# Keys of the memory for the second layer: from a one-pass float32 product to three float32r passes over split rows

## The chip, the cores and the metric

The kernel runs on one core of a Trainium2 chip. The metric is the device time of one execution in microseconds (us). The five parts of the core that the profile shows are PE (matmul, with its weight loads as PEld), DVE, ACT, POOL, and the queue of SP, which issues most of the DMAs.

## What is computed

The reference is an encoder trunk of two layers over 256 rows of 1024 channels. The first layer mixes by a bidirectional state-space layer (S5) with a gated linear unit behind it, the second by dilated attention. Each layer then attends into 256 rows of a memory, with normalised queries and keys, and ends with an MLP:

```python
for i in range(DEPTH):                       # DEPTH = 2
    hn = rms_norm(h, norm_mix[i])
    h = h + (s5_mixer(hn, ...) if i % 2 == 0 else dilated_attention_mixer(hn, ...))
    h = h + memory_cross_attention(rms_norm(h, norm_xattn[i]), rms_norm(mem, norm_mem[i]), ...)
    h = h + sq_relu_mlp(rms_norm(h, norm_mlp[i]), mlp_w1[i], mlp_w2[i])
# in memory_cross_attention, mem_n is the normalised memory:
kv = (mem_n @ w_kv).reshape(bsz, mlen, 2, MEM_HEADS, MEM_HEAD_DIM)
k = rms_norm(kv[:, :, 0], g_k)
v = kv[:, :, 1]
```

The products `mem_n @ w_kv` of both layers depend on the memory alone. There are four of them, each 256 x 1024 by 1024 x 1024: keys and values of layer 0, keys and values of layer 1.

## The kernel before

The four products are written by `memory_part(layer, q, ...)`, where q is 0 for keys and 1 for values. It has two ways to multiply. With one operand tile it calls `gemm32` (L240 to L252): plain float32 matmuls of 128x512 at L248, 32 of them for one product, each of which the trace shows as two records. The weights come by `weight_raw` (L234) into the pool of four `raw` tiles. With two operand tiles, a high and a low part in float32r, it calls `gemm`: per half of a weight block (256 rows of 512 columns) `weight_half` loads the same `raw` tile (L193), ACT casts it to `whi` (L161), DVE makes the rest `wlo` (L162), and `unit_mms` issues twelve matmuls of 128x512, three for each operand block: high by high (L207), high by low (L208), low by high (L209). One product is 96 such matmuls and eight halves.

The order of the program is this. First comes the S5 stage, in eight chunks. In each, DVE makes input weights (`s5_weigh_in`, transposed by PE at L1042 and copied by ACT at L1044), PE drives the states (`drive`, L1081), DVE scans them (`scan`, L1096 to L1113, with decays R that ACT writes at L1091 and L1092), ACT copies them (L1116, L1117), PE makes impulse responses (`impulse`, L1144, from `wk`, which ACT fills at L1135 to L1138; the result `kx` goes to DRAM at L1154 and comes back as M at L1160, issued from ACT's queue), and `read` multiplies states, W and M (L1173, L1176), applies a gelu (G, L1179) and transposes (L1185). Behind the S5 stage, still under its PSUM pools, stand `load_gains` (L121), `bias_rows` (L483 to L496, with two small matmuls at L489, its copies at L490, and DMAs on SP's queue), the load of x, and three products in plain float32: keys of layer 0, values of layer 0, keys of layer 1.

Then the PSUM pools change from two, five and one banks to four and four. In the new ones the transposed memory rows of layer 1, `mT[1]`, are split into the two tiles `mp` (pool `m1`). The values of layer 1 follow in three passes, then the gated unit (`glu`). The keys of each layer are normalised by `key_norms` (L350 on ACT, L354 on POOL), which the `hook` calls after each half of the values; the keys of layer 0 are transposed (L379) during the gated unit's first part, those of layer 1 only in the first cross attention.

Tile, the framework, orders each engine's instructions when the program is built: those written earlier go first, and those written later fill in where the earlier ones can't run yet and where their buffers are free. So the float32 products, written behind the S5 stage, stand between its instructions in PE's order. Pools on a stack reuse each other's memory: `m1` lies where the pool `s5` lay, and the split weights `whi` and `wlo` (pool `wq`) partly where the pool `s5m` lay. In the built program the instructions that first write `mp` wait for the last matmul of the S5 stage that reads from `s5`, and the first cast to `whi` waits for the last users of `s5m`.

Of the kernel before, what the change touches and what calls it, by code (L numbers as in the profile page):

```python
# [1251 lines left out]
def trunk(tc, a, stages=("s0", "x0", "m0", "d1", "x1", "m1")):  # L1252
    with ExitStack() as ctx:
        k = Trunk(ctx, tc, a)
        nc = tc.nc
        seq = [q for q in ("s0", "x0", "m0", "d1", "x1", "m1") if q in stages]
        first = {"x": "norm_xattn", "m": "norm_mlp", "d": "norm_mix"}
        xin = lambda: nc.sync.dma_start(k.h, a["x"][0].rearrange("(t p) c -> p t c", p=P))

        def store(nb):  # L1260
            for t in range(2):
                cs = slice(nb * 512, (nb + 1) * 512)
                (nc.sync, nc.scalar)[t].dma_start(a["out"][t * P:(t + 1) * P, cs], k.h[:, t, cs])

        after = {}
        for n, q in enumerate(seq):
            after[q] = k.norm_after(first[seq[n + 1][0]], int(seq[n + 1][1])) if n + 1 < len(seq) else \
                (store, None)
        late = ("norm_mix", "norm_xattn", "norm_mlp", "xattn_q_gain", "attn_q_gain", "attn_k_gain")
        early = ("norm_mem", "xattn_k_gain")  # L1270
        kvp0 = tc.alloc_tile_pool(name="kv0", bufs=1)
        right = lambda n: ctx.enter_context(tc.tile_pool(name=n, bufs=1, side="right"))
        krp = tc.alloc_tile_pool(name="kr", bufs=1)
        kv = [[krp.tile([P, 2, D], F32, name="k%d" % q), (kvp0, right("v1"))[q].tile([P, 2, D], F32, name="v%d" % q)]
              for q in range(2)]
        keys = [None, None]
        if "s0" in seq:
            kvt = tc.alloc_tile_pool(name="kvt", bufs=1)
            with k.banks(2, 5, 1):
                with tc.tile_pool(name="s5", bufs=1) as ph:  # L1280
                    with tc.tile_pool(name="s5p", bufs=1) as pr:
                        k.load_gains(pr, early, nc.sync)
                        k.s5_load(pr, kv[0][1], kv[1])
                        k.s5_params(pr)
                        mT = [k.memory_in(0, kvt, kv[0][1])]
                        k.s5_norm(ph, kv[0][0].rearrange("p a b -> p (a b)"))
                        k.s5_tables(ph)
                        k.s5_b(ph)
                        turns = k.s5_turns(pr, ph, k.h.rearrange("p t c -> p (t c)"))
                        k.s5_weigh_in(ph, 0)  # L1290
                        k.s5_c(ph, pr)
                        k.s5_skip(ph, pr)
                        k.s5_input(ph)
                        mr = k.row_rstd(kv[0][1], "mem")
                        mT.append(k.memory_in(1, kvt, kv[0][1]))
                    gT = k.new_x()
                    with tc.tile_pool(name="s5m", bufs=1) as mp:
                        k.s5(mp, ph, turns, gT)
                        k.load_gains(mp, late, nc.sync)
                        k.bias_rows()  # L1300
                xin()
                k1 = right("k1")
                k.wq = right("wq")
                k0 = tc.alloc_tile_pool(name="k0", bufs=1, side="right")
                k.memory_part(0, 0, kv[0][0], mT[:1], mr, k.kvw)
                k.memory_part(0, 1, kv[0][1], mT[:1], mr)
                k.memory_part(1, 0, kv[1][0], mT[1:], mr)
        else:
            with k.banks(4, 4), tc.tile_pool(name="kvt", bufs=1) as kvt:
                k.load_gains(kvt, early, nc.sync)  # L1310
                k.load_gains(kvt, late, nc.sync)
                k.bias_rows()
                mem = kvt.tile([P, 2, D], F32, tag="mem", name="mem")
                k.memory_load(mem)
                mr = k.row_rstd(mem, "mem")
                k1 = right("k1")
                k.wq = right("wq")
                k0 = tc.alloc_tile_pool(name="k0", bufs=1, side="right")
                for q in range(2):
                    if "x%d" % q in seq:  # L1320
                        mT = [k.memory_in(q, kvt, mem)]
                        for i in range(2):
                            k.memory_part(q, i, kv[q][i], mT, mr)
                        keys[q] = k.key_parts(q, k.key_norms(q, kv[q][0], kvt), (k0, k1)[q])
                xin()
        with k.banks(4, 4):
            if "s0" in seq:
                m1 = tc.alloc_tile_pool(name="m1", bufs=1)
                parts = [m1.tile([P, KT, S], F32R, tag="mp%d" % q, name="mp") for q in range(2)]
                for q in (slice(0, 4), slice(4, 8)):  # L1330
                    k.split(parts[0][:, q], parts[1][:, q], mT[1][:, q])

                kn = {}

                def norms(nb):
                    kn[nb] = k.key_norms(nb, kv[nb][0], k0)

                k.memory_part(1, 1, kv[1][1], parts, mr, hook=norms)
                k.glu(gT, after["s0"][0], lambda: keys.__setitem__(0, k.key_parts(0, kn[0], k0)))
                m1.release()  # L1340
                kvt.release()
                st = after["s0"][1]
            else:
                done, st = k.norm_after(first[seq[0][0]], int(seq[0][1]))
                done(0)
                done(1)
            krp.release()
            for q in seq:
                done, nst = after[q]
                L = int(q[1])  # L1350
                if q[0] == "x":
                    with tc.tile_pool(name="xa", bufs=1) as ph:
                        def fill():
                            if q == "x0" and "s0" in seq:
                                keys[1] = k.key_parts(1, kn[1], k1)

                        vals = [ph.tile([P, 2, D], F32R, tag="v%d" % i, name="vp") for i in range(2)]
                        k.memory_attention(L, st["x"], st["r"], (keys[L], vals, kv[L][1]), done, ph, fill)
                    if L == 0:
                        k0.release()  # L1360
                        kvp0.release()
                elif q[0] == "m":
                    k.mlp(L, st["x"], st["r"], done)
                elif q[0] == "d":
                    k.dilated_attention(st["x"], st["r"], done)
                st = nst if q[0] != "s" else st
        if "x0" not in seq:
            k0.release()
            kvp0.release()
# [25 lines left out]
```

## Time and profile before

| what | us |
| --- | --- |
| median of 3 runs (lowest to highest) | 1068.58 (1065.11 to 1069.62) |
| the profiled execution, its own time | 1063.82 |
| its span, first to last instruction | 1062.0 |
| PE busy in the span | 1009.4 (95%) |
| DVE, ACT, POOL busy | 693.7, 576.6, 211.2 |

The mean granted clock of TensorE over the span is 0.988. The page divides the span by engine; the timeline gives instructions in order of time, merged where they repeat; a window row gives the stretch, its length, the busy time of PE, PEld, DVE, ACT and POOL with the number of instructions in brackets, the granted clock (1.00 is 2.4 GHz, 0.50 is 1.2 GHz), the busy share of the DMA engines and the GB/s that they moved. In a timeline the columns are start, duration, engine, line, operation, destination and sources, count, and in square brackets the idle time before it with what ended it. Times count from the span's start.

### The profile page before, as it was taken

How to read it: one execution, taken by the hardware profiler on the slowest of the kernel's cores; microseconds unless marked ns; L12 is line 12 of the kernel's file. 1: busy time of each engine (PE TensorE's matmuls, PEld its weight loads, DVE VectorE, ACT ScalarE, POOL GpSimd, SP SyncE). 2: the span in 40 equal slices, each digit the busy share in tenths (PEclk: the TensorE clock that was granted, in tenths of full speed). 3: DMA queues.
4: the chain of work that ended last, by engine and by line, in shares of the span. 5: the costliest groups of instructions: out<-in, count | busy, mean ns of one | idle time of the engine just before them, and what ended most of it. 6: DMA issues, size and time to landing. Idle time of an engine off the chain costs nothing. (4 is left out here: it accounts for less than half of the span.)

```text
span 1062.0 us, 17010 instructions
## 1 busy us (share of the span) xinstructions
PE 1009.4 (95%) x6591; PEld 829.6 (78%) x6591; DVE 693.7 (65%) x1108; ACT 576.6 (54%) x1030; POOL 211.2 (20%) x186
## 2 busy tenths in 40 slices
PE   4878889989999999999989999999999999999998
PEld 4545446568898988999778878878788989889996
DVE  7889996366686645444667777778747775544444
ACT  7545444675675644444545656667535655444443
POOL 3999880030000110000220030000200001100000
PEclk9999899999999999999999999999999999999999
DMA  9322233465533455555555555554325244555552
GB/s 197 106 90 71 64 125 104 153 209 178 172 129 130 169 187 175 190 191 181 178 179 179 159 168 178 157 163 141 127 90 174 104 156 163 178 190 188 188 186 101
DMA packets 98429, 163.80 MB, mean 154 GB/s; under 512 B 16704, under 2 KB 27116, under 8 KB 98092
## 3 DMA queue, kind: packets, MB, share of 16 engines
q1 hardware_dynamic: 89052, 158.84, 47.5%
q10 hardware_dynamic: 9296, 3.87, 1.4%
q8 instruction: 52, 0.85, 0.3%
q14 instruction: 29, 0.24, 0.1%
HBM read 160.70 MB, written 3.83 MB: 155 GB/s over the span
## 5 line engine op out<-in xcount | busy, mean ns | idle before, releaser
L162 DVE TENSOR_TENSOR wlo<-raw,whi 128x1024 fp32r<-128x1024 f32 x264 | 331.1, 1255 | 237.4 <-ACT whi L161 233.9
L161 ACT CAST whi<-raw 128x1024 fp32r<-128x1024 f32 x264 | 276.7, 1048 | 225.9 <-PE psa L209 143.0
L207 PE MATMUL psa<-whi,xs 128*128 128x512 f32 x448 | 178.2, 398 | 0.5 <-ACT sg L1220 0.5
L209 PE MATMUL psa<-whi,xs 128*128 128x512 f32 x448 | 177.2, 396 | 0.0
L208 PE MATMUL psa<-wlo,xs 128*128 128x512 f32 x448 | 176.9, 395 | 0.0
L292 POOL TENSOR_TENSOR sq<-rl 128x512 f32<-128x512 f32 x32 | 40.1, 1252 | 531.5 <-ACT rl L291 531.5
L279 PE MATMUL psb<-xs,whi 128*128 128x256 f32 x512 | 145.1, 283 | 0.0
L281 PE MATMUL psb<-xs,whi 128*128 128x256 f32 x512 | 145.0, 283 | 0.0
L283 PE MATMUL psb<-xs,wlo 128*128 128x256 f32 x512 | 144.9, 283 | 0.0
L209 PE MATMUL psa<-whi,hl 128*128 128x512 f32 x256 | 101.6, 397 | 0.0
L208 PE MATMUL psa<-wlo,hh 128*128 128x512 f32 x256 | 101.5, 397 | 0.0
L207 PE MATMUL psa<-whi,hh 128*128 128x512 f32 x256 | 101.4, 396 | 0.0
L248 PE MATMUL psa<-raw,mT 128*128 128x512 f32 x192 | 95.1, 639 | 5.7 <-ACT k L334 5.7
L279 PEld LDWEIGHTS psb<-xs,whi 128*128 128x128 f32 x512 | 98.2, 192 | 0.9 <-DVE xs L184 0.4
L281 PEld LDWEIGHTS psb<-xs,whi 128*128 128x128 f32 x512 | 98.2, 192 | 0.5
L283 PEld LDWEIGHTS psb<-xs,wlo 128*128 128x128 f32 x512 | 98.3, 192 | 0.0
L207 PEld LDWEIGHTS psa<-whi,xs 128*128 128x128 f32 x448 | 84.5, 189 | 17.0 <-ACT sg L1220 0.9
L209 PEld LDWEIGHTS psa<-whi,xs 128*128 128x128 f32 x448 | 84.6, 189 | 16.6
L208 PEld LDWEIGHTS psa<-wlo,xs 128*128 128x128 f32 x448 | 84.6, 189 | 15.9
L248 PEld LDWEIGHTS psa<-raw,mT 128*128 128x128 f32 x192 | 36.6, 202 | 44.3 <-issue 36.9
L209 PEld LDWEIGHTS psa<-whi,hl 128*128 128x128 f32 x256 | 48.2, 188 | 11.6
L208 PEld LDWEIGHTS psa<-wlo,hh 128*128 128x128 f32 x256 | 48.3, 189 | 11.1
(330 smaller groups left out, 1537.5 us busy)
## 6 DMA issues: line engine op xcount, KB each, us to landing
raw<-in_mlp_w SPq DMA_DIRECT2D x128, 512.0 KB, 4.3
raw<-in_attn_w_qkv SPq DMA_DIRECT2D x72, 512.0 KB, 3.6
raw<-in_xattn_w_kv SPq DMA_DIRECT2D x32, 512.0 KB, 3.8
raw<-in_s_w_glu SPq DMA_DIRECT2D x16, 512.0 KB, 4.3
raw<-in_xattn_w_q SPq DMA_DIRECT2D x16, 512.0 KB, 3.4
raw<-in_xattn_w_o SPq DMA_DIRECT2D x16, 512.0 KB, 3.4
raw<-in_attn_w_o SPq DMA_DIRECT2D x8, 512.0 KB, 3.4
bias_d<-bias_o SPq DMA_DIRECT2D x1, 1536.0 KB, 9.6
```

Source lines behind the costliest of these rows:

```text
L161: self.nc.scalar.copy(hi, src)
L162: self.nc.vector.tensor_sub(lo, src, hi.bitcast(F32))
L207: nc.tensor.matmul(acc[t], xh[:, k0 + k, sl], hi[:, k % 2, :], start=st, stop=False)
L208: nc.tensor.matmul(acc[t], xh[:, k0 + k, sl], lo[:, k % 2, :], start=False, stop=False)
L209: nc.tensor.matmul(acc[t], xl[:, k0 + k, sl], hi[:, k % 2, :], start=False, stop=en)
L248: nc.tensor.matmul(acc[t], xT[:, k + q, t * P:(t + 1) * P], raw[:, q, :], start=k + q == 0, stop=k + q == KT - 1)
L279: nc.tensor.matmul(o, hi[:, k % 2, fs], xh[:, kt, :], start=st, stop=False, skip_group_check=True)
L281: nc.tensor.matmul(o, hi[:, k % 2, fs], xl[:, kt, :], start=False, stop=False, skip_group_check=True)
L283: nc.tensor.matmul(o, lo[:, k % 2, fs], xh[:, kt, :], start=False, stop=en, skip_group_check=True)
L292: nc.gpsimd.tensor_mul(sq, rl, rl)
```

## The change

The call that computes the keys of layer 1 moves from the end of the S5 block to the place just ahead of the values of layer 1, and its operand changes from `mT[1:]` (one tile, so `gemm32`) to `parts` (the two tiles `mp`, so `gemm`). Nothing else is edited.

```diff
                 k.memory_part(0, 0, kv[0][0], mT[:1], mr, k.kvw)
                 k.memory_part(0, 1, kv[0][1], mT[:1], mr)
-                k.memory_part(1, 0, kv[1][0], mT[1:], mr)
         else:
@@
                 def norms(nb):
                     kn[nb] = k.key_norms(nb, kv[nb][0], k0)
 
+                k.memory_part(1, 0, kv[1][0], parts, mr)
                 k.memory_part(1, 1, kv[1][1], parts, mr, hook=norms)
                 k.glu(gT, after["s0"][0], lambda: keys.__setitem__(0, k.key_parts(0, kn[0], k0)))
                 m1.release()
```

## Rows read from the trace of the kernel before

**Rows 1.** The page: busy time by engine, and the chain that ended last

```profile
PE 1009.4 (95%) x6591; PEld 829.6 (78%) x6591; DVE 693.7 (65%) x1108; ACT 576.6 (54%) x1030; POOL 211.2 (20%) x186
...
PE 28%; DVE 0%; ACT 0%; issue 0%
```

**Rows 2.** Windows of 20 us around the end of the S5 stage

```profile
160.00:180.00 20.00, 20.00 (x207) 11.33 (x204) 11.54 (x20) 6.93 (x15) 0.10 (x1) 0.94 0.35 99
180.00:200.00 20.00, 20.00 (x189) 11.17 (x189) 6.97 (x12) 7.42 (x13) 0.00 (x0) 1.00 0.39 119
200.00:220.00 20.00, 16.91 (x65) 11.10 (x64) 10.68 (x14) 19.45 (x52) 3.75 (x2) 1.00 0.67 215
```

**Rows 3.** L248 in one window (PE and PEld columns only), then PE's timeline

```profile
154.90:203.45 48.55, 29.50 (x64) 11.51 (x64) 0.96 0.36 113
...
163.18 6.17 PE L248 MATMUL psa<-raw,mT 128*128 128x512 f32 x14
...
172.95 5.42 PE L248 MATMUL psa<-raw,mT 128*128 128x512 f32 x12
...
185.71 9.71 PE L248 MATMUL psa<-raw,mT 128*128 128x512 f32 x22
195.35 0.45 PE L1173 MATMUL psb<-W,xs 128*64 128x64 f32 x8
...
197.66 0.33 PE L1176 MATMUL psb<-M,u 64*64 64x64 f32 x4
```

**Rows 4.** ACT's timeline (ACTq is its queue issuing DMAs) through the tail

```profile
164.14 1.08 ACT L1044 COPY VT<-psb 128x512 f32<-128x512 f32 x2
...
169.47 2.52 ACTq L1160 DMA_DIRECT2D M<-kd  x4
173.07 0.38 ACT L1179 ACTIVATE G<-psb 128x256 f32<-128x256 f32 x1 [3.16 <-PE psb L1176]
...
179.03 0.37 ACT L1189 CAST xs<-psb 128x256 fp32r<-128x256 f32 x1 [4.22 <-PE psb L1185]
...
181.01 0.68 ACT L334 ACTIVATE k<-psa,rmem 128x512 f32<-128x512 f32 x1
...
190.13 1.04 ACT L1117 COPY xs<-xt 64x1024 f32<-64x1024 f32 x1
...
198.51 1.99 ACT L161 CAST mp<-mT 128x1024 fp32r<-128x1024 f32 x2
...
203.86 0.28 ACT L490 COPY junk<-psb 24x160 f32<-24x160 f32 x1 [0.21 <-PE psb L489]
```

**Rows 5.** DVE's timeline: the scan of the last chunk

```profile
170.54 0.69 DVE L1096 TENSOR_TENSOR tmp<-psb,xs 128x512 f32<-128x512 f32 x1 [3.17 <-issue]
...
181.82 1.23 DVE L1105 TENSOR_TENSOR_SCAN psb<-R,psb 128x512 f32<-128x512 f32 x1 [1.97 <-ACT R L1092]
...
188.36 0.68 DVE L1113 TENSOR_TENSOR xt<-tmp,psb 128x512 f32<-128x512 f32 x1
```

**Rows 6.** PE's timeline: first and last of 96 matmuls, values of layer 1

```profile
204.78 0.50 PE L207 MATMUL psa<-whi,mp 128*128 128x512 f32 x1 [0.95 <-ACT k L334]
...
215.85 0.40 PE L209 MATMUL psa<-whi,mp 128*128 128x512 f32 x1
...
233.77 0.40 PE L209 MATMUL psa<-whi,mp 128*128 128x512 f32 x1
```

**Rows 7.** DVE's timeline: one split alone, one beside POOL's L354

```profile
199.64 1.23 DVE L162 TENSOR_TENSOR mp<-mT,mp 128x1024 fp32r<-128x1024 f32 x1 [10.60 <-ACT mp L161]
...
216.95 2.77 DVE L162 TENSOR_TENSOR wlo<-raw,whi 128x1024 fp32r<-128x1024 f32 x1 [2.37 <-ACT whi L161]
```

**Rows 8.** Two windows behind an idle time of PE, then the instruction that ended it

```profile
64.00:66.00 2.00, 2.00 (x6) 0.49 (x8) 0.24 (x1) 1.35 (x3) 1.84 (x3) 0.50 0.00 0
66.00:68.00 2.00, 2.00 (x86) 1.93 (x90) 0.00 (x0) 0.00 (x0) 1.93 (x2) 0.77 0.03 8
...
63.92 2.08 PE L248 MATMUL psa<-raw,mT 128*128 128x512 f32 x2 [5.74 <-ACT k L334]
```

## The prediction, written before the changed kernel was run

> **What bounds the kernel now.** Start at the page's busy shares: PE is at 95%, and the chain that ended last consists of PE work alone [rows 1]. The mean hides stages, so the next view is windows around the place of the edit. From 160 to 200 us PE is busy in every microsecond while DVE and ACT are half idle or worse; from 200 to 220 PE has holes and ACT is at 19.45 of 20 [rows 2]. That says that PE bounds the tail of the S5 stage, but not with what. The third view is one line alone: in 154.90 to 203.45 there are 64 records of L248, and 64 is one whole float32 product [rows 3]. As the products go in the order of the code, these are the keys of layer 1: all the work that the change removes lies here, as filler between S5 instructions, and it is what makes PE look full. Each stretch of filler delays the S5 instruction behind it, though: 22 records stand in front of the last `read` [rows 3]. So two questions decide: how much of the tail is filler that closes up, and what then is late in its place (the fourth view, the timelines of ACT and DVE there) [rows 4, 5].
>
> **Part 1, what is removed.** A run of 22 records takes 9.71 us, so one takes 0.442 at full clock [rows 3], and 64 take 28.3. Four evictions of 0.68 us on ACT (L334) leave the tail too [rows 4]. This is a ceiling; the S5 chain sets what comes back:
> - The drive of the last chunk stands behind 14 records (6.17 us) [rows 3]. Its input on ACT is there at 164.14 + 1.08 = 165.2 [rows 4], so it could run at 165.2, but DVE works at the previous scan until 3.17 us before 170.54, that is 167.4 [rows 5]: 3.1 gained at the scan's start.
> - The scan's second part waits for R [rows 5], which ACT writes behind G and L1189. G can't go before ACT's queue has issued M, at 169.47 + 2.52 = 172.0: 1.1 gained. Then L1185 no longer stands behind 12 records (5.42 us) [rows 3]; ACT waited 4.22 for it [rows 4]. Behind the freed wait come the same copies, and one eviction of 0.68 less. In all 1.1 + 4.2 + 0.7 = 6.0: the second part of the scan starts at about 175.8 instead of 181.82, and the states' copies end at 185.2 instead of 190.13 + 1.04 = 191.2 [rows 4, 5].
> - The last `read` began at 195.35, 4.2 us after those copies, since 22 records stood ahead of it [rows 3]. That 4.2 closes up.
>
> In sum the S5 stage ends 6.0 + 4.2 = 10.2 us earlier, its last matmul at 187.8 instead of 198.0 [rows 3]; the other 18.1 us of filler turn into idle PE. This assumes the same order on ACT. The best order would let R be written early, and DVE alone set the pace: scan from 167.4, six operations of up to 0.69 us to 171.5, then the 188.36 + 0.68 - 181.82 = 7.2 us of [rows 5], two copies of 1.04 [rows 4], the 2.6 us of `read` [rows 3]: end at 183.4, a gain of 14.6. The worst I allow is 8. No loss, since nothing is added to this stretch.
>
> **Part 2, the clock.** [rows 8] show what idle PE costs afterwards: after a pause of 5.74 us the granted clock is 0.50 (1.2 GHz) from 64 to 66 and 0.77 on average in the next window, and two records of L248 take 2.08 us in place of 0.88; that is 3 us at half rate. With the filler gone, PE has such pauses throughout the tail. The last `read` (2.6 us at full clock) and transposes run partly at half: +1 on the path (0 to 3). The three-pass product starts behind a thin stretch, with 3 us at half rate as in [rows 8], in which 1.5 us of work is lost: +1.5 (0 to 2).
>
> **Part 3, what is added.** The 48 matmuls of a half product went from 204.78 to 215.85 [rows 6]: 11.07 us for 47 steps, 0.236 each; 96 are 22.6 us. The Trainium skill ("TensorE: Matmul & The Clock Gate", Back-to-back issue gap) has the columns at 2.4 GHz and 2.5 ns more, 0.216 for 512 columns; by that estimate the passes take 20.7 and the sum is 1.9 lower. The row is this kernel's own work, so it stands. When can they start? Their operand `mp` and the split weights lie in memory of the S5 pools, so, as in the kernel before, the cast to `mp` comes 0.5 us after the last `read` (198.0 to 198.51) [rows 3, 4]; these passes can't fill the tail as the float32 product did. PE's first L207 came at 204.78, released by the keys' eviction [rows 6]. Without that eviction the next late thing is `bias_rows`, the last user of the old PSUM banks, whose copy ends at 203.86 + 0.28 = 204.1, 6.1 us after the last `read` [rows 4]. The split is ready by then. So the start is 6.1 instead of 6.8 us behind the S5 stage: -0.7. Its 28.3 us cover is replaced by no cover: all 22.6 us lie on PE's path.
>
> **Part 4, splits and queues.** Eight more casts (1.05 us) and eight more DVE remainders (1.23 us alone, 2.77 beside POOL's key multiplication [rows 7]) stand on ACT and DVE. Twelve matmuls take 2.8 us, which covers either; the work runs ahead by three buffers. Uncovered, each half would cost up to 2.3 us, 18 in all, but the first 48 matmuls of the values ran with no gap at this load [rows 6]. SP's queue issues the same eight loads of weights, no DMA more; they come now behind the `bias_rows` DMAs or just ahead of them, with four tiles loaded long before, because their buffers are free as soon as layer 0's values end. POOL gets no instruction. The values of layer 1 took 234.0 - 204.8 = 29.2 us, of which 22.6 are matmuls and 1.6 key transposes; 5.0 is waiting, in the stretch where ACT is full with the norms of both layers' keys [rows 2, 6]. With two products to spread that over I expect 2.5 of waiting for both: -2.5, between -5 (all hidden) and +2 (two of the slow DVE remainders exposed).
>
> **Sum.** -10.2 + 1.0 + 1.5 - 0.7 + 22.6 - 2.5 = +11.7 us. Everything behind (`glu` on) only moves. On the profiled execution that is 1063.8 + 11.7 = 1075.5. The median of the runs lies 4.8 above that execution, so I put the sum on the median: 1080. The bounds: -14.6 + 0 + 0 - 0.7 + 22.6 - 5 = +2, and -8 + 3 + 2 - 0.7 + 22.6 + 2 = +21.
>
> **Rivals.**
> - Tail closes fully (faster). PE is the bound and 28.3 us go and 22.6 come: -28.3 - 0.7 + 22.6 - 2.5 = -9, so 1060. It decides if the S5 chain on ACT and DVE can run 28 us faster. For it: PE is full from 160 to 200 [rows 2]. Against: even DVE alone allows 14.6; the break-even is a tail shorter by 19.4. A rule of the Trainium skill points here ("Perfetto Trace Analysis", Identifying the Most-Contended Engine): relieve the engine with the highest occupancy. The section behind it (Optimization Strategy) also says that interleaving stages with different limits pays, which speaks against the change; the rows side with that. Chance 0.05.
> - Same time: the three passes do find their way into the tail. If the memory of `mp` came free with the last impulse at about 176, PE would have the last two `read`s and small matmuls (9 us) and 22.6 to do from there, with a start of 1.5: 209 instead of 204.8, less 2.5 of waiting, +2, so 1070. Against: the place of the cast [rows 4]. Chance 0.10.
> - Slower still: the clock stays at 0.50 through the sparse tail and the ACT order gets no better: -8 + 3 + 2 + 22.6 - 0.7, waiting unchanged: +19, so 1087. For it [rows 8]. Chance 0.15.
>
> **How the numbers follow.** The forecast has 0.70, with about 0.06 of it below +5.3. A measurement of this kernel can tell 0.5% from no change, 5.3 us. Faster 0.05; same 0.16; slower 0.79. The range leaves out the fast rival, half of the same-time one and the ends of the others: 1070 to 1088.
>
> **What would show it.** No L248 after about 155; the S5 stage's last L1176 near 188; holes in PE and a granted clock of 0.5 between 165 and 190; the first L207 about 6 us behind that L1176, then 192 matmuls on `mp` in some 48 us, ending near 245 instead of 234. The prediction is wrong if L207 on `mp` stands among S5 matmuls, if the last L1176 is at 180 or earlier, or if PE waits for `whi` or `wlo` at most halves.

## The result, and the profile after

| what | before | changed |
| --- | --- | --- |
| median (lowest to highest), us | 1068.99 (1065.11 to 1069.62) | 1080.69 (1079.16 to 1085.37) |
| ratio of the changed kernel to the one before | | 1.0122, 95% interval 1.0088 to 1.0156 |
| span of the profiled execution, us | 1062.0 | 1083.6 |
| PE, DVE, ACT busy, us | 1009.4, 693.7, 576.6 | 1020.9, 705.6, 586.0 |

The kernel became 11.7 us slower by the medians and 13.0 by the ratio (9.4 to 16.7 by its interval). The spans stand 21.6 us apart, since the profiled execution of before was a quick one and that of the changed kernel its slowest; so stretches are compared below and not spans. First the page of the changed kernel: busy time, and the chain that ended last, which answer to [rows 1].

```profile
PE 1020.9 (94%) x6623; PEld 849.9 (78%) x6623; DVE 705.6 (65%) x1116; ACT 586.0 (54%) x1038; POOL 212.1 (20%) x186
...
PE 28%; DVE 0%; ACT 0%; issue 0%
```

PE's share hardly moves (95% to 94%), and the chain at the end is the same; it covers 28% of the span, all of it after 700 us, so in neither kernel does it say anything of the place of the edit. The page doesn't show what happened; the windows do. Same columns as [rows 2]:

```profile
160.00:180.00 20.00, 12.68 (x186) 10.16 (x186) 15.38 (x26) 7.94 (x17) 4.23 (x4) 0.62 0.19 59
180.00:200.00 20.00, 14.09 (x162) 10.23 (x161) 7.96 (x14) 7.53 (x14) 0.00 (x0) 0.50 0.06 14
200.00:220.00 20.00, 17.12 (x61) 12.94 (x61) 11.16 (x13) 15.70 (x39) 4.21 (x2) 0.77 0.70 223
220.00:240.00 20.00, 20.00 (x87) 16.10 (x86) 10.47 (x11) 14.48 (x25) 3.37 (x3) 1.00 0.58 188
```

From 160 to 200 PE was full at a clock of 0.94 and 1.00; now it is busy 12.68 and 14.09 of 20, at 0.62 and 0.50. No L248 runs there any more. From 220 on PE is full where it had holes; the kernel before had this in its window:

```profile
220.00:240.00 20.00, 18.16 (x80) 14.10 (x80) 15.04 (x18) 13.58 (x21) 4.72 (x2) 1.00 0.59 193
```

Now PE's timeline through the tail and behind it, which answers to [rows 3] and [rows 6]:

```profile
153.87 0.33 PE L1081 MATMUL psb<-u,VT 64*64 64x64 f32 x4 [1.14 <-ACT VT L1044]
...
171.12 0.33 PE L1081 MATMUL psb<-u,VT 64*64 64x64 f32 x4 [2.80 <-DVE xt L1112]
...
186.84 1.12 PE L1185 MATMUL psb<-ident,G 128*64 128x64 f32 x16 [0.48 <-ACT G L1179]
192.85 0.69 PE L1173 MATMUL psb<-W,xs 128*64 128x64 f32 x8 [4.89 <-issue]
...
196.57 0.48 PE L1176 MATMUL psb<-M,u 64*64 64x64 f32 x4
...
204.10 0.80 PE L207 MATMUL psa<-whi,mp 128*128 128x512 f32 x1 [1.19 <-ACT junk L490]
204.69 0.63 PE L208 MATMUL psa<-wlo,mp 128*128 128x512 f32 x1
...
251.30 0.39 PE L207 MATMUL psa<-whi,xs 128*128 128x512 f32 x1
```

The rows to see: the last drive (L1081) starts 17.25 us behind the one before it; PE idles 4.89 us ahead of the last `read`; each of the read's instructions takes half as long again (0.69 for 0.45); the three passes can't start before the last bias copy, and from 204.10 to 251.30 no row of the 192 matmuls on `mp` shows a wait. ACT's timeline, for [rows 4]:

```profile
177.78 0.38 ACT L1179 ACTIVATE G<-psb 128x256 f32<-128x256 f32 x1 [3.38 <-PE psb L1176]
...
188.01 0.37 ACT L1189 CAST xs<-psb 128x256 fp32r<-128x256 f32 x1 [1.22 <-PE psb L1185]
188.09 2.52 ACTq L1160 DMA_DIRECT2D M<-kd  x4
190.65 1.04 ACT L1116 COPY xs<-xt 64x1024 f32<-64x1024 f32 x1 [2.27 <-DMA M<-kd]
191.71 1.04 ACT L1117 COPY xs<-xt 64x1024 f32<-64x1024 f32 x1
...
197.56 1.04 ACT L161 CAST mp<-mT 128x1024 fp32r<-128x1024 f32 x1
```

And DVE's, for [rows 5]:

```profile
181.79 2.34 DVE L1105 TENSOR_TENSOR_SCAN psb<-R,psb 128x512 f32<-128x512 f32 x2 [1.00 <-ACT R L1092]
...
187.41 0.68 DVE L1113 TENSOR_TENSOR xt<-tmp,psb 128x512 f32<-128x512 f32 x1
```

The scan ends at 187.41 + 0.68 = 188.09; the copies of its result start at 190.65, behind the issue of M's four DMAs. In the kernel before that issue was over (188.72) when the scan ended (189.04), and the copies waited for DVE alone:

```profile
186.20 2.52 ACTq L1160 DMA_DIRECT2D M<-kd  x4
189.08 1.04 ACT L1116 COPY xs<-xt 64x1024 f32<-64x1024 f32 x1 [2.88 <-DVE xt L1113]
```

The last cast in ACT's rows of the changed kernel is that to `mp`, 0.5 us behind the last `read` as before.

To compare kernels whose clocks ran differently early on, one anchor serves: the drive of the last chunk but one (L1081). From there the text measures four stretches: *tail*, to the end of the last `read` (L1176); *start*, from there to the first matmul on `mp`; *block*, from there to the gated unit's first matmul (L207 on `xs`); *gate*, to the first transpose of the rows behind it (L177). All in us, from PE's timelines:

| kernel | anchor at | tail | start | block | gate | sum |
| --- | --- | --- | --- | --- | --- | --- |
| before | 148.83 | 49.16 | 6.79 | 29.22 | 25.24 | 110.41 |
| before, a second profile | 155.89 | 47.69 | 6.79 | 29.22 | 25.26 | 108.96 |
| changed | 153.87 | 43.18 | 7.05 | 47.20 | 26.71 | 124.14 |
| changed, a second profile | 154.54 | 41.95 | 7.05 | 46.24 | 26.65 | 121.89 |
| changed, a third profile | 154.63 | 42.54 | 7.05 | 47.53 | 26.66 | 123.78 |
| no keys at all | 156.27 | 39.95 | 7.06 | 30.70 | 26.67 | 104.38 |
| float32 at the new place | 156.11 | 42.44 | 6.61 | 56.04 | 26.65 | 131.74 |
| both products | 145.94 | 49.15 | 6.78 | 50.11 | 24.98 | 131.02 |
| half the filler added | 156.07 | 45.00 | 7.06 | 46.43 | 26.65 | 125.14 |
| half and half | 149.68 | 45.77 | 7.06 | 37.63 | 26.65 | 117.11 |
| norms later | 154.83 | 47.73 | 6.79 | 27.45 | 28.68 | 110.65 |
| M issued from SP | 154.26 | 40.50 | 7.06 | 46.85 | 26.69 | 121.10 |

(For float32 at the new place, *start* and *block* count from its first L248.) Over these stretches the change costs 13.7 us in the first pair of profiles and 12.9 in the second, and 11.5 to 15.2 by which two profiles are paired.

### The profile page after: what moved, and what is told of

Its sections match the earlier page's. It is cut to its first block, busy times and chain, and to the rows that moved or that the text cites. A ratio compares the mean times of both kernels' runs of the same rounds, so it can differ in the third digit from the quotient of the medians.

```text
span 1083.6 us, 17104 instructions
## 1 busy us (share of the span) xinstructions
PE 1020.9 (94%) x6623; PEld 849.9 (78%) x6623; DVE 705.6 (65%) x1116; ACT 586.0 (54%) x1038; POOL 212.1 (20%) x186
## 5 line engine op out<-in xcount | busy, mean ns | idle before, releaser
L162 DVE TENSOR_TENSOR wlo<-raw,whi 128x1024 fp32r<-128x1024 f32 x272 | 341.0, 1255 | 248.6 <-ACT whi L161 246.4
L161 ACT CAST whi<-raw 128x1024 fp32r<-128x1024 f32 x272 | 284.8, 1048 | 235.9 <-PE psa L209 153.0
L207 PE MATMUL psa<-whi,xs 128*128 128x512 f32 x448 | 179.3, 400 | 0.7 <-ACT sg L1220 0.7
L207 PE MATMUL psa<-whi,hh 128*128 128x512 f32 x256 | 101.5, 396 | 0.0
L207 PEld LDWEIGHTS psa<-whi,xs 128*128 128x128 f32 x448 | 85.1, 190 | 17.2 <-ACT sg L1220 1.2
L209 PEld LDWEIGHTS psa<-whi,xs 128*128 128x128 f32 x448 | 84.9, 189 | 16.7
L248 PE MATMUL psa<-raw,mT 128*128 128x512 f32 x128 | 67.3, 671 | 3.9 <-ACT k L334 3.9
L209 PEld LDWEIGHTS psa<-whi,hl 128*128 128x128 f32 x256 | 48.3, 188 | 11.5
L207 PEld LDWEIGHTS psa<-whi,hh 128*128 128x128 f32 x256 | 48.3, 189 | 11.0
```

Of the source, the lines that this page charges most:

```text
L161: self.nc.scalar.copy(hi, src)
L162: self.nc.vector.tensor_sub(lo, src, hi.bitcast(F32))
L207: nc.tensor.matmul(acc[t], xh[:, k0 + k, sl], hi[:, k % 2, :], start=st, stop=False)
L209: nc.tensor.matmul(acc[t], xl[:, k0 + k, sl], hi[:, k % 2, :], start=False, stop=en)
L248: nc.tensor.matmul(acc[t], xT[:, k + q, t * P:(t + 1) * P], raw[:, q, :], start=k + q == 0, stop=k + q == KT - 1)
```

## The experiments

**What the keys of layer 1 cost in the kernel before.** This kernel leaves out that product: the norms of layer 1's keys read the keys of layer 0.

```diff
-                    kn[nb] = k.key_norms(nb, kv[nb][0], k0)
+                    kn[nb] = k.key_norms(nb, kv[0][0], k0)
-                k.memory_part(1, 0, kv[1][0], parts, mr)
```

> The changed kernel without any product for the keys of layer 1 (that part of the computation is left out; their norms read the keys of layer 0 instead, so the work behind the product stays). Theory of the prediction (place): the product was filler in the tail of the S5 stage and mostly rode in PE's idle time there, so leaving it out gives back only what the tail closes by, 5 to 10 us, and some waiting: about 8 us under the kernel before, 1061 (1057 to 1064). Against the changed kernel that is about 20 us less, the whole price of the 96 matmuls on the path. Rival (PE is the bound and every record counts): 28 us under the kernel before, 1041.

Measured: 1064.20 us, 0.9958 (0.9937 to 0.9979) of before, which had 1069.37 in that batch, just above the range expected. 28.3 us of PE work cost the kernel before 5 us. That is the strongest reading of the study: most of the filler was free. A rule of the Trainium skill ("Perfetto Trace Analysis", Identifying the Most-Contended Engine) would have one relieve the engine of highest occupancy first; here that engine was PE, at 20.00 of 20 in [rows 2], and relieving it of the whole product brought a fifth of its time. The same section of the Trainium skill has the headroom of TensorE judged not by matmul time but by the share of peak work and by the weight loads' busy share; in [rows 2] the weight loads are at 11.33 and 11.17 of 20, beside 11.54 for DVE in the first window, so the section points at PE less plainly than the prediction's rival had it. And the three passes cost 1080.69 - 1064.20 = 16.5 us behind the tail, against those 5.

**The place, without the three passes.** The product stays float32, but moves as the change has it.

```diff
-                k.memory_part(1, 0, kv[1][0], parts, mr)
+                k.memory_part(1, 0, kv[1][0], mT[1:], mr)
```

> One part of the change alone: the keys of layer 1 are computed at the new place, but still by the plain float32 product from the unsplit rows. Theory of the prediction (the place costs, the passes save): 64 records of 0.442 us are 28.3 on PE's path where the passes took 22.6, less some waiting for splits: 2 to 6 us above the changed kernel, about 1085. Rival (the passes and their splits on ACT and DVE are what costs): near the kernel before, 1069.

Measured: 1089.54 us, 1.0213 (1.0185 to 1.0241). PE's timeline:

```profile
205.16 29.21 PE L248 MATMUL psa<-raw,mT 128*128 128x512 f32 x64 [0.71 <-ACT junk L490]
243.08 0.50 PE L207 MATMUL psa<-whi,mp 128*128 128x512 f32 x1 [0.32 <-ACT whi L161]
245.87 0.80 PE L208 MATMUL psa<-wlo,mp 128*128 128x512 f32 x1 [2.28 <-DVE wlo L162]
```

The move alone costs 20.2 us against the 1069.37 of its batch, and the changed kernel is 8.8 us quicker than this one. In the first profile its block is 8.8 us shorter too. Of these, 3.8 lie ahead of the values: 28.65 us here from the first L248 to the first L207, and 22.4 + 2.4 for the 96 matmuls with their start at half clock. The other 5.0 lie in the values themselves, which take 27.4 us here, not 22.4, and wait for splits again. So the change's arithmetic is a gain, and its place a loss.

**The three passes added, the filler left.** A dead float32 product (its output is overwritten) stays at the old place; the new call is there as well.

```diff
                 k.memory_part(0, 1, kv[0][1], mT[:1], mr)
+                k.memory_part(1, 0, kv[1][1], mT[1:], mr)
```

> The other part alone: the changed kernel with the old float32 product kept at its old place as filler (its result is overwritten by the values). Theory of the prediction: the tail is as long as before, with the clock up, and the 96 matmuls lie behind it: before + 22.6 less 2.5 of waiting, about 1089 (1085 to 1092), so that the changed kernel's gain from the shorter tail shows as the 5 to 10 us between this and it. Rival (what the tail lost to the half clock is as much as it gained by the missing filler): the same as the changed kernel, 1081.

Measured: 1091.73 us, 1.0219 (1.0179 to 1.0258). The tail is 49.15, inside the 47.69 to 49.16 of the kernel before, so the shorter tail of the changed kernel comes from the filler's absence and not from the new call. The windows:

```profile
160.00:180.00 20.00, 20.00 (x220) 11.11 (x220) 10.09 (x17) 8.48 (x17) 0.00 (x0) 1.00 0.42 120
180.00:200.00 20.00, 20.00 (x139) 10.00 (x137) 8.78 (x16) 7.90 (x12) 0.00 (x0) 1.00 0.32 98
```

With the filler PE's clock is 1.00 throughout. Taking the filler out of this kernel, which gives the changed one, is worth 11 us by the medians; the stretches show 7 to 9 of these (131.02 against 121.89 to 124.14). The tail has 6 to 7.2, the block 2.6 to 3.9, with a wait of 2.11 us for POOL that the changed kernel lacks, and the gate gives 1.7 back. So filler of 28 us costs 5 to 11 here, by what stands beside it, and not 28.

**Half the filler.** To tell the length of the tail from its clock, a dead half product goes to the old place. (`memory_part` gets an argument `half` that keeps one of its two column blocks.)

```diff
                 k.memory_part(0, 1, kv[0][1], mT[:1], mr)
+                k.memory_part(1, 0, kv[1][1], mT[1:], mr, half=0)
```

> The changed kernel with the first half (512 columns) of the old float32 product kept at its old place as filler (its result is overwritten): 32 records, none of them ahead of the last read. Theory of the prediction: the filler delays G, R and the scan as it did before, but no longer the last read; tail of 45 to 47 us from the drive of chunk 6, and a time 1 to 5 us above the changed kernel, about 1084. Rival (the clock at half rate is what the tail mostly lost, and filler keeps it up): the same as the changed kernel or faster, 1076 to 1081, with the granted clock above 0.9 up to the last read.

Measured: 1086.03 us, 1.0176 (1.0153 to 1.0199). Windows around the place where the filler ends:

```profile
160.00:180.00 20.00, 16.82 (x213) 9.94 (x211) 16.90 (x28) 8.79 (x19) 6.05 (x5) 1.00 0.42 131
180.00:187.00 7.00, 7.00 (x48) 3.24 (x48) 0.63 (x2) 2.71 (x7) 0.00 (x0) 1.00 0.25 78
187.00:200.00 13.00, 6.71 (x119) 5.25 (x118) 6.61 (x11) 4.35 (x8) 0.00 (x0) 0.79 0.20 59
```

The clock is 1.00 until 187, and yet the tail is 45.0 and not below 42. Filler that keeps the clock up delays the S5 instructions by more than the clock gives back. The rival, that the clock is the main loss and a little filler would pay for itself, falls. The median is 5.3 us above that of the changed kernel, which ran in another batch, where 1 to 5 were expected.

**Half and half.** Half of the product as float32 filler at the old place, half in three passes at the new one.

```diff
                 k.memory_part(0, 1, kv[0][1], mT[:1], mr)
+                k.memory_part(1, 0, kv[1][0], mT[1:], mr, half=0)
@@
-                k.memory_part(1, 0, kv[1][0], parts, mr)
+                k.memory_part(1, 0, kv[1][0], parts, mr, half=1)
```

> Half of layer 1's keys (the first 512 columns) as one float32 product at the old place, the other half in three passes at the new place. Theory (the tail of the S5 stage gives back less than the filler that leaves it, and each half moved behind it costs its own 11.2 us): tail from the last drive to the last read 44 to 46 us as with half the filler, 144 matmuls on the split memory in 34 to 37 us, the time about 1074 (1070 to 1078), half way between before and changed or a little above. Rival: the loss is mainly that PE's clock falls in a tail without filler; then half the filler, which keeps the clock up to about 187 us, brings nearly the whole of the shorter tail, and the time is at or below 1069.

Measured: 1076.81 us, 1.0072 (1.0046 to 1.0098), between both kernels. The tail (45.77) is as forecast; the block is 37.63, 0.6 above, with one wait of 1.45 us for a split. Half the change costs 7.9 us of the whole change's 11.7: the one point between that was tried isn't better than the kernel before.

**The three passes as filler.** The rival of the prediction that put the passes into the tail: the split rows and weights go into memory that is free there, under the old PSUM pools.

```diff
+                 parts = [kvt.tile([P, KT, S], F32R, tag="mT0", name="mp"),
+                          k1b.tile([P, KT, S], F32R, tag="kT1", name="mp")]
...
+                 k.early_keys(kv[1][0], parts, mr, v1p.tile([P, 2, D], F32R, tag="v1", name="ws"))
```

> Three passes at the old place: the split rows and one pair of split weights lie in memory that is free before the S5 stage ends (the slot of the rows of layer 0, the slot of the values of layer 1, and 8 KB a partition beside the S5 pools), under the old PSUM pools. In the built order 33 of the 96 matmuls stand ahead of the last transposes of the S5 stage and 12 more ahead of the bias rows. Theory (the operands' memory, not the passes, kept the product out of the tail): those 45 matmuls, 10.6 us, leave the path, part of it paid back by splits on ACT and DVE beside the S5 chain: 4 to 10 us under the changed kernel, about 1074. Rival (the tail has no room for this work, ACT and DVE set it): the same as the changed kernel or slower, 1081 to 1086.

Measured: 1082.18 us, 1.0141 (1.0092 to 1.0189), where 1074 was expected. The four runs lie far apart, at 1077.41, 1078.04, 1086.32 and 1086.43, and the profile is that of the 1086.32; so the median shows none of the forecast gain of 4 to 10 us, while a gain of some 3 us over the changed kernel is neither shown nor excluded. In this kernel the lines are numbered some 17 higher, and the passes are L407. ACT's timeline:

```profile
182.30 0.61 ACT L161 CAST mp<-mT 128x512 fp32r<-128x512 f32 x1
```

PE's:

```profile
187.18 2.93 PE L407 MATMUL psa<-ws,mp 128*128 128x512 f32 x6
...
193.89 1.18 PE L407 MATMUL psa<-ws,mp 128*128 128x512 f32 x4 [0.39 <-DVE ws L162]
```

Only 18 of the 96 matmuls run ahead of the last `read`, the first at 187.18. The casts to `mp` stand at 182.3 in ACT's order, though ACT had idle stretches ten us earlier, and the split of each half needs ACT and DVE, which the S5 chain uses too. The tail took 46.1 us, 3 to 4 more than in the changed kernel, and 2.2 to 3.4 of that lie ahead of the last drive, before any pass ran. Float32 needs no split: it takes raw weights. That this is why it was the better filler is argued from this one order; whether a better order of the casts would fill the tail wasn't tried.

**The start.** Gains and bias rows written ahead of the S5 chunks, so that the passes need not wait for the last bias copy (L490).

```diff
-                        k.s5(mp, ph, turns, gT)
                         k.load_gains(mp, late, nc.sync)
                         k.bias_rows()
+                        k.s5(mp, ph, turns, gT)
```

> The changed kernel with the gains and the bias rows written ahead of the S5 chunks. Theory of the prediction: without the filler the bias rows set the start of the passes, 7.05 us behind the last read; with them gone the splits do (cast of the rows, cast and remainder of the first weights), 4.5 to 6 us. The time falls by 1 to 2 us against the changed kernel, about 1079, unless the other order of the S5 chunks costs it. Rival (the splits are as late): no shorter gap.

Measured: 1086.46 us, 1.0191 (1.0164 to 1.0219). PE's timeline:

```profile
207.74 1.22 PE L207 MATMUL psa<-whi,mp 128*128 128x512 f32 x2 [2.36 <-ACT whi L161]
```

The start fell from 7.05 to 4.02 us (4.5 to 6 expected), and what is next is the cast to `whi`, as predicted. But the time went up where 1079 was expected: the moved rows changed the order of the S5 instructions, the tail took 47.0 and the clock was 0.50 from 150 to 210. One cannot read the price of the start from the total here; only from its stretch.

**The early part.** The first profiles had the anchor at 148.83 and 153.87. Is that a cost of the change? Each kernel was looked at once more.

> The kernel before once more, for a second profile of it. Question: how much of the difference between the two profiles at hand lies in stretches where the two programs are the same. Counted from the drive of chunk 6 to the last read of the S5 stage, I expect 49 us, as in the first profile (49.2); the start of that drive itself may lie anywhere from 145 to 156 us, by what clock the first chunks were granted.

> The changed kernel once more, for a second profile of it. From the drive of chunk 6 to the last read I expect 40 to 43 us (43.2 in its first profile, and 40.0 to 42.4 in the two kernels without filler so far), and the drive itself anywhere from 145 to 156 us, as in the kernel before. If the drive lies at 153 or later again, and at 149 or earlier in the kernel before, the change costs time ahead of the place that it edits, which the prediction does not have.

Measured: 1069.35 and 1084.01 us. PE's timelines, the kernel before first:

```profile
155.89 1.57 PE L1081 MATMUL psb<-u,VT 64*64 64x64 f32 x64 [1.36 <-ACT VT L1044]
...
203.25 0.33 PE L1176 MATMUL psb<-M,u 64*64 64x64 f32 x4
210.37 0.50 PE L207 MATMUL psa<-whi,mp 128*128 128x512 f32 x1 [0.95 <-ACT k L334]
```

```profile
154.54 1.57 PE L1081 MATMUL psb<-u,VT 64*64 64x64 f32 x64 [1.36 <-ACT VT L1044]
...
196.01 0.48 PE L1176 MATMUL psb<-M,u 64*64 64x64 f32 x4
203.54 0.80 PE L207 MATMUL psa<-whi,mp 128*128 128x512 f32 x1 [1.18 <-ACT junk L490]
```

The kernel before can have its anchor at 155.89 as well, so the early shift isn't the change's. The tail is 47.69 against 41.95, and start, block and gate agree with the first pair to 1 us; the kernel before is 1.3 below the 49 expected, the changed kernel inside its range.

**Where the values' waiting comes from.** In the kernel before, the block took 29.22 us, of which 5 to 6 is waiting. Here the norms of layer 1's keys move from the values' block into the gated unit.

```diff
-                k.memory_part(1, 1, kv[1][1], parts, mr, hook=norms)
+                k.memory_part(1, 1, kv[1][1], parts, mr, hook=lambda nb: norms(0) if nb == 0 else None)
...
+                    keys[0] = k.key_parts(0, kn[0], k0)
+                    with tc.issue_after(k.last_evac.ins):
+                        norms(1)
```

> The kernel before, with the norms of layer 1's keys moved on ACT behind the last eviction of layer 1's values (behind the first key transposes), those of layer 0's keys where they were. It asks where the 5.0 us of waiting in the values' block of the kernel before come from (29.2 us, of which 22.6 are matmuls and 1.6 key transposes). Theory: from ACT, which is full there with the norms of both layers' keys; with half of them gone the block takes 25 to 27 us instead of 29.2 and the time falls by 2 to 4 us, to about 1066. Rival: the loads of the later weights wait in SP's queue behind the bias rows, or the split is too slow by itself; then the block stays within 1 us of 29.2 and the time within 2 us of before. If the norms are merely late behind the values, the block is shorter but the first layer's gates wait for them, and the time is the same.

Measured: 1070.05 us, 1.0008 (0.9988 to 1.0029), no change. PE's timeline in the gated unit:

```profile
254.43 0.50 PE L207 MATMUL psa<-whi,xs 128*128 128x512 f32 x1 [0.51 <-ACT whi L161]
255.69 0.50 PE L208 MATMUL psa<-wlo,xs 128*128 128x512 f32 x1 [0.76 <-DVE wlo L162]
263.31 0.50 PE L207 MATMUL psa<-whi,xs 128*128 128x512 f32 x1 [2.06 <-ACT sg L1220]
```

The block fell by 1.8 us, the gate grew by 3.4. The norms' waiting isn't lost by moving them, it goes along, and 2.8 us of it shows in these three rows (0.52 of the last was there before). So ACT's norms are part of the waiting, but the theory's 2 to 4 us aren't there, and in the block ACT now waits for late raw weights:

```profile
219.83 1.05 ACT L161 CAST whi<-raw 128x1024 fp32r<-128x1024 f32 x1 [2.06 <-DMA raw<-in_xattn_w_kv]
```

That is the third outcome named beforehand: the block is shorter, the gates wait for the norms, and the time is the same. Of the rival the late weights are there, though the block fell by more than its 1 us. In the changed kernel the waiting is gone; that this is so because two products lie beside the same norms is argued from the table.

**What kept the tail from closing further.** In the changed kernel the last state copies wait 2.27 us behind the issue of M's four DMAs on ACT's queue, with the scan long done. Here these four issues, of the last chunk only, go to SP's queue; on PE, DVE and POOL the order of instructions is the same.

```diff
-                nc.scalar.dma_start(m[16 * s_:16 * s_ + 16].rearrange("c (q j) x -> c q j x", q=2), src)
+                (nc.sync if ch == 7 else nc.scalar).dma_start(m[16 * s_:16 * s_ + 16].rearrange("c (q j) x -> c q j x", q=2), src)
```

> The changed kernel, with the four DMA issues of the last chunk's M moved from ACT's queue to SP's; PE, DVE and POOL keep their order, and ACT's differs by that one line. In the changed kernel the last chunk's state copies (L1116, L1117) waited 2.27 us behind these issues, which stood behind a late L1189, while the scan had long ended. Theory (the tail closed by 6.0 us in place of 10.2 because G's way through PE at half clock makes L1189 late, and the issues of M then stand ahead of the copies): the copies start within 0.3 us of the scan's end, the last read ends 2 to 2.5 us earlier, 39.5 to 41 us behind the last but one drive instead of 42 to 43.2, and the time falls by 2 to 2.5 us, to about 1078.5. Rival: the last read waits for the impulse M or for the next thing on ACT, and the tail and the time stay within 0.7 us of the changed kernel's.

> The changed kernel once more, beside the run with M's issues on SP's queue on the same chip. Tail from the last but one drive to the last read 41.9 to 43.2 us, copies waiting 2.2 to 2.3 us for M's issue, time 1079 to 1083.

Measured on the same chip: 1079.98 us with the issues on SP, 1.0102 (1.0079 to 1.0126) of before; 1081.35, 1.0117 (1.0092 to 1.0143), for the changed kernel. With the issues on SP, SP's timeline:

```profile
186.25 2.58 SPq L1160 DMA_DIRECT2D M<-kd  x4
```

ACT's:

```profile
188.09 0.37 ACT L1189 CAST xs<-psb 128x256 fp32r<-128x256 f32 x1 [1.22 <-PE psb L1185]
188.36 1.04 ACT L1116 COPY xs<-xt 64x1024 f32<-64x1024 f32 x1
```

PE's:

```profile
190.56 0.69 PE L1173 MATMUL psb<-W,xs 128*64 128x64 f32 x8 [2.51 <-issue]
```

The copy stands right behind L1189, PE's idle time ahead of the last `read` falls from 4.89 to 2.51, and the tail from 42.54 to 40.50, as the theory says. The sum of the four stretches falls by 2.7 us. The means of six runs each differ by 1.6, give or take 1.5: a gain below the 2 to 2.5 forecast, though not clear of it, and its size can't be told better from these runs. The Trainium skill ("DMA: Bandwidth & Descriptors", Issuing engines are not separate DMA queues) has it that another issuing engine saves only the issuing sequencer's own time; here that time was the 2.52 us of the L1160 row, and it lay on the path.

## Why the prediction was right, and where its terms were off

The time came out at 1080.7 for a forecast of 1080.0, slower as forecast. The mechanism holds: filler that was mostly free was replaced by work with no cover. That the medians are 11.7 us apart, the very sum of the prediction, is luck: the ratio gives 13.0, and the stretches give 13.7 and 12.9. Its terms, from the first pair of profiles, with those from the second pair where they differ:

| term | forecast | measured |
| --- | --- | --- |
| S5 tail, with its own clock loss | -10.2 + 1.0 = -9.2 | -6.0 (-5.7) |
| start behind the last `read` | -0.7 | +0.3 |
| 96 more matmuls | +22.6 | +22.4 |
| half clock at the passes' start | +1.5 | +2.4 (+1.4) |
| waiting in the block | -2.5 | -5.6 |
| gated unit, without the moved transposes | 0 | +0.25 |
| sum | +11.7 | +13.7 (+12.9) |

The sum came within 2.0 us (1.2), because errors of 3.2, 1.0 and 0.9 us on one side stood against 3.1 on the other; that they nearly cancel is luck as well.

- *The tail was mis-sized.* The steps, measured from the anchor: the last drive came 3.2 us earlier, but its 64 matmuls then take 2.5 us for 1.2, most of them at half clock, and the scan behind it started 2.0 earlier (19.66 us behind the anchor for 21.71), where 3.1 was forecast. G came 0.3 earlier, not 1.1, since four reads at half clock take 4.2 us for 2.6. The second part of the scan came 5.1 earlier (27.92 us behind the anchor for 32.99), forecast 6.0, and the scan ended 6.0 earlier. Up to there the working held. The state copies, though, ended only 3.5 earlier: the prediction carried the 6.0 through to them unchanged, and left out that in ACT's queue L1189 and M's issue stand between. In the kernel before those were done ahead of the scan's end, and the copies waited for DVE. Now L1189 comes only 2.9 us earlier (34.14 behind the anchor for 37.00), with reads and L1185 at half clock ahead of it, and M's issue then blocks the copies for 2.5 us: a wait that took the place of the one removed. Moving the issue brought back 2.0 of it. The 4.2 us of filler ahead of the last `read` closed as forecast (to 0.1 us), and the read's own slow-down was 1.6 rather than 1.0.
- *The clock.* In the second window the granted clock was 0.50 throughout, the level at 1.2 GHz, where the prediction allowed for part of it. The kernel with no keys, whose S5 instructions are the same, had 0.67 there in its profile, and its rows bear on what that is worth:

```profile
186.01 0.38 ACT L1179 ACTIVATE G<-psb 128x256 f32<-128x256 f32 x1 [1.93 <-PE psb L1176]
187.18 0.37 ACT L1189 CAST xs<-psb 128x256 fp32r<-128x256 f32 x1 [0.78 <-PE psb L1185]
```

  L1189 stands 30.9 us behind its anchor, against 34.1 and 32.9 in the changed kernel, and the tail is 39.95, shorter by 9.2 us than in the first profile of before and by 7.7 than in the second, with 9.2 forecast. Part of the difference lies ahead of that stretch: the last drive stands 15.66 us behind the anchor there, and 17.25 and 16.01 in the changed kernel. Behind the drive L1189 comes 1.6 earlier than in both. That the clock makes those 1.6 is argued from these three profiles; no run held the clock fixed.
- *The start.* The prediction named what would be late next (the bias copy, L490), and the row says so (`1.19 <-ACT junk L490`). But the two L489 and the copy were taken at the durations of before; at half clock the first L489 takes 1.47 for 0.82. The copy behind it came 3.5 us after the last `read` for 2.7, and the last copy stands behind three casts to `whi` in ACT's order (200.94 to 203.87).
- *The 96 matmuls* are 0.2335 us each at full clock, as in the kernel before, and nothing covers them: 192 x 0.2335 = 44.8, plus 2.4 for the start, is the whole block of 47.20. The estimate that the prediction worked out from the Trainium skill ("TensorE: Matmul & The Clock Gate", Back-to-back issue gap), 0.216 each and 20.7 in all, is too low by the 1.7 that the rows have more. That section of the Trainium skill gives the figure for a matmul by itself, and about 0.131 for a stream of weight loads and matmuls; the rows are above both.
- *The waiting* went altogether; the prediction had half of it and gave all of it as its bound. The norms of layer 0's keys and the splits now lie beside 44.8 us of matmuls rather than 22.4; all sixteen transposes moved into the gated unit, which had five of them before (1.2 us for the other eleven, where the prediction had 1.6; counted out of both rows of the table).
- *The rivals.* A tail that closes fully is excluded by the kernel without keys: even with nothing in their place the time is 1064, not 1041. The passes as filler (1070 by the rival) came to 1082 in their own experiment, though with runs from 1077 to 1086. The place of the cast wasn't all that held them back, as the prediction thought: with the memory free only 18 of 96 ran in the tail. That ACT's and DVE's order held the others is argued. Of the slower rival the clock at 0.50 was there and the tail came near its 8 less 3; but the waiting vanished, so 1087 wasn't reached.
- *What would show it:* no L248 after 155, holes and a clock of 0.50, and 192 matmuls in 47.2 us came as written. The last L1176 ended at 197.05, not near 188; 5.0 us of that are the later anchor, the rest the tail's miss; the last matmul on `mp` stands at 251, not near 245, with the later anchor as the largest part.
- *Two readings that were too strong.* DVE was at 11.54 of 20 in the window from 160 [rows 2], which isn't half idle. And the chain that ended last [rows 1] lies far behind the edit, so it said nothing of the tail; the windows carried that step.

## What to carry to other kernels

Price filler by what its removal gives back on the chain that it covers, not by its busy time: 28.3 us of PE work cost 5 us here, so a form of it that takes 22.4 us at an uncovered place couldn't pay. What filled PE's gaps here was work that asks little of the other engines: float32 matmuls on raw weights did, while three passes with splits on ACT and DVE hardly did in the one order tried. And where an engine's queue also issues DMAs, a chain that becomes quicker in one place meets these issues in another: follow the chain through the queue's order instruction by instruction, not by one shift for all that stands behind a step.

## What the runs showed of the hardware

The instructions ahead of the anchor are the same in both kernels, and yet it lies anywhere from 145.94 to 156.27 us in the twelve profiles of the table. What differs is the granted clock in the early chunks; that it makes the whole shift is argued from the windows below. They go from 90 to 100 us, first the kernel before, whose anchor lay at 148.83:

```profile
90.00:100.00 10.00, 10.00 (x74) 4.98 (x73) 8.52 (x13) 4.64 (x10) 9.61 (x9) 0.96 0.28 80
```

Its second profile, with the anchor at 155.89:

```profile
90.00:100.00 10.00, 10.00 (x69) 5.66 (x68) 5.81 (x11) 5.71 (x10) 9.69 (x9) 0.57 0.04 14
```

And the kernel with both products, with the anchor at 145.94:

```profile
90.00:100.00 10.00, 10.00 (x73) 4.98 (x73) 8.66 (x13) 4.82 (x10) 9.69 (x9) 0.94 0.29 80
```

So one profile against one other can be up to 10 us off by the early chunks alone, nearly as much as this change costs; a step is better measured from an anchor just ahead of it.
